# Ln and Exp of the first four rows done row by row instead of in pairs

## The chip, the cores and the metric

The kernel runs on one core of one Trainium2 chip. The metric is the device time of one execution in microseconds (us). Five runs of the kernel before gave a median of 169.43 us, from 169.14 to 169.55. A separate execution was recorded by the hardware profiler; it took 169.62 us.

## The reference

For every row of 1024 positive numbers the sum of the reciprocals is computed, over 32 x 512 rows:

```python
x: float32 [32, 512, 1024], |normal| + 1e-6
return np.sum(1.0 / x, axis=-1).astype(np.float32)
```

## The kernel before

The 16384 rows are spread over 128 partitions, 128 rows in each. What the kernel calls "row r" is therefore a tile of 128 x 1024 numbers, one matrix row in each partition, 512 KB. Rows 0 to 125 are treated whole; the last two, 126 and 127, are cut into two parts each, numbered 126 to 129.

The reciprocal is not computed element by element. A row has two halves a and b of 512 numbers. The kernel forms the product p = a b, then 1/p by two instructions on ScalarE, Ln with a scale and Exp of the negative, and uses 1/a + 1/b = (a + b) / (a b). So Ln and Exp run over 512 numbers per row rather than 1024. The steps of a row are tokens in a written-out plan (PLAN, line 37), a letter with the row's number. `+2` after it means two rows in one instruction, a pair, called a chain of two rows; `@` gives a slot or a bank. In the order of a row's life:

- **D** (line 185, SyncE's queue): loads so many further rows into a ring of 40 rows in SBUF. `D12 D15 D13` load rows 0 to 39 at the start. Every later load overwrites ring rows, and so waits until their readers and writers are done.
- **P** (line 197, GpSimd): the product of the halves, into a slot of the tile `prod` (22 slots of 512 numbers).
- **C** and **V** (lines 207 and 218): for some rows TensorE copies half b into a PSUM bank (matmul with the identity), and VectorE multiplies half a with it. This is the product without GpSimd. **W** is the same by VectorE alone.
- **S** (line 230, TensorE): adds the two halves into a PSUM bank, by two matmuls with the identity. Only for some rows.
- **L** (line 240, ScalarE): Ln of the product with scale 2^17, in place in its slots. `L0+2@0` treats rows 0 and 1 and sets their slots to 0 and 1; P and V read the slots from these tokens.
- **E** (line 249, ScalarE): Exp of minus that. With a bank, as in `E0+2@6`, the result goes to PSUM (here banks 6 and 7); without one it stays in its slot.
- **R** (line 265, VectorE): multiplies and sums. If the row has an S, it multiplies the sum in PSUM with 1/p in `prod` (128 x 512). Otherwise it multiplies both halves in the ring with 1/p in PSUM (128 x 1024). Each R is followed by a short instruction that reads out the accumulator, and the profile shows the two under the same line.

The order of tokens in the plan is the order of each engine's instructions; there is no other scheduler. Between engines the function `note` (line 133) records which ring rows, slots and banks each instruction reads and writes, and drops a wait where another wait already implies it.

For the first rows this means: rows 0 and 1 have P0+2 on GpSimd, and no S, so E0+2 writes to PSUM banks 6 and 7 and R0 and R1 read them there. Row 2 has P2 on GpSimd, row 3 has C3 and V3; both have an S (banks 0 and 1), so E2+2 stays in its slots. The next pair, rows 4 and 5, uses banks 6 and 7 again: E4+2@6 must wait until R0 and R1 have read them.

Of the kernel before, what the change touches and what calls it, by code (L numbers as in the profile page):

```python
# [11 lines left out]
def kernel(  # L12
# [22 lines left out]


    PLAN = """
        D12 D15 D13 P0+2 C3@3 S2@0 V3 P2 L0+2@0 C11@3 S3@1 E0+2@6 P4+2 V11 L2+2@2 R0 S6@2
        E2+2 R1 P6+2 L4+2@4 R2 R3 E4+2@6 S7@0 P8+2 L6+2@8 R4 S10@1 E6+2 R5 D7 P10 L8+2@10 R6
        R7 S11@2 E8+2@6 L10+2@6 R8 E10+2 R9 R10 R11 P12+2 C19@3 S14@0 V19 P14+2 L12+2@12  # L40
        S15@1 E12+2@6 S18@2 R12 P16+2 L14+2@16 R13 E14+2 R14 P18 L16+2@18 R15 S19@0 E16+2@6
        P20+2 L18+2@14 R16 D10 S22@1 E18+2 R17 P22+2 L20+2@20 R18 R19 E20+2@6 S23@2 P24+2
        L22+2@0 R20 S26@0 E22+2 R21 D7 P26 L24+2@2 R22 C27@3 R23 E24+2@6 P28+2 S27@1 V27 R24
        L26+2@4 C35@3 R25 E26+2 P30+2 S30@2 L28+2@8 V35 R26 E28+2@6 R27 S31@0 P32+2 L30+2@10
        R28 E30+2 S34@1 R29 D8 P34 L32+2@12 R30 R31 P36+2 E32+2@6 S35@2 L34+2@6 R32 C43@3
        E34+2 R33 P38+2 S38@0 L36+2@16 R34 R35 E36+2@6 S39@1 V43 P40+2 L38+2@18 R36 S42@2
        E38+2 R37 D8 P42 L40+2@20 R38 R39 E40+2@6 S43@0 P44+2 L42+2@14 R40 S46@1 E42+2 R41
        D4 L44+2@0 R42 R43 E44+2@6 P46+2 C51@3 R44 S47@0 V51 P48+2 L46+2@2 R45 S50@2 E46+2
        R46 P50 L48+2@8 R47 S51@1 E48+2@6 P52+2 L50+2@4 R48 S54@0 E50+2 R49 D6 P54+2 C59@3
        L52+2@10 R50 R51 E52+2@6 S55@2 V59 P56+2 L54+2@12 R52 S58@1 E54+2 R53 D6 P58  # L50
        L56+2@16 R54 R55 S59@0 E56+2@6 P60+2 L58+2@6 R56 S62@2 E58+2 R57 D4 P62+2 L60+2@18
        R58 R59 C67@3 E60+2@6 P64+2 S63@0 L62+2@20 V67 R60 E62+2 S66@1 R61 D4 P66 L64+2@14
        R62 E64+2@6 P68+2 R63 S67@2 L66+2@0 R64 E66+2 S70@0 R65 D3 P70+2 L68+2@2 R66 R67
# [259 lines left out]
```

## Time and profile before

| what | us |
|---|---|
| median of five runs (lowest, highest) | 169.43 (169.14, 169.55) |
| the profiled execution, its whole time | 169.62 |
| its span in the trace | 167.6 |
| TensorE busy | 132.1 |
| VectorE busy, 283 instructions | 128.2 |
| ScalarE busy, 157 instructions | 132.8 |
| GpSimd busy | 128.0 |
| load queue, share of 16 DMA engines' span | 94.6% |
| bytes read from HBM | 67.11 MB |

Busy time is the time in which an engine executes something. No engine's share of the span is over 79%, and the page lists for each group of instructions the idle time ahead of it and what ended it. The chain of waits follows the work that ended last back to the start; a releaser is inferred from semaphore events. Starts are counted from the beginning of the span, and lengths of successive instructions of one engine may overlap, so the distance of two starts is shorter than the length of the first.

### The profile page before, as it was taken

Reading aid. Unit: us, or ns where it says so; the run is one execution under the profiler, and the core shown is the slowest. Engines: PE = TensorE matmul, PEld = TensorE weight load, DVE = VectorE, ACT = ScalarE, POOL = GpSimd, SP = SyncE. Lnnn points to the kernel's source line nnn. Section 1 sums busy time; section 2 is a strip of 40 time slices with the busy share of each in tenths; the row PEclk is TensorE's granted clock in tenths of the full one; section 3 lists DMA queues with packets and bytes.
Section 4 is the critical chain, followed back from the end, with each engine's and each line's share of the span. In section 5 each row is a group of like instructions: output and inputs, shape, how many; then the busy total and the mean of one; then the engine's idle time right before and its main releaser. Section 6 shows DMA issues by size and latency. Waiting matters only on the chain.

```text
span 167.6 us, 1329 instructions
## 1 busy us (share of the span) xinstructions
PE 132.1 (79%) x292; PEld 54.6 (33%) x292; DVE 128.2 (76%) x283; ACT 132.8 (79%) x157; POOL 128.0 (76%) x80
## 2 busy tenths in 40 slices
PE   0000699929979999977998999999799679989691
PEld 0000243214433434322433434344244133434260
DVE  0000139853789989887798898799999999999993
ACT  3000096916999999976999997999899999999992
POOL 1000699129999999949999997966899997979960
PEclk9999999978999999999999999999999999999999
DMA  5998999999998998999999999999999999999910
GB/s 188 481 457 375 469 469 469 396 404 470 419 407 370 426 473 385 459 403 433 437 430 430 446 407 450 411 436 434 393 434 429 415 435 409 423 408 408 391 55 16
DMA packets 4615, 67.25 MB, mean 401 GB/s; under 512 B 512, under 2 KB 640, under 8 KB 2176
## 3 DMA queue, kind: packets, MB, share of 16 engines
q1 hardware_dynamic: 4608, 67.18, 94.6%
q8 instruction: 2, 0.03, 0.1%
q14 instruction: 5, 0.04, 0.1%
HBM read 67.11 MB, written 0.07 MB: 401 GB/s over the span
## 4 chain that ended last, share of the span: by engine, by line
DMA 50%; DVE 17%; POOL 11%; issue 8%; PE 8%; ACT 4%; DVEq 0%; SPq 0%; ACTq 0%; POOLq 0%
DMA ring<-in_x_dram 50%; POOL prod L197 11%; DVE ring L265 10%; PE ps L230 5%; DVE prod L265 4%; PE ps L207 3%; DVE prod L218 2%; ACT prod L240 2%; ACT ps L249 1%; DVE sums L265 1%; ACT prod L249 1%; DVEq L308 0%; SPq L185 0%; ACTq L240 0%; POOLq L197 0%
## 5 line engine op out<-in xcount | busy, mean ns | idle before, releaser
L197 POOL TENSOR_TENSOR prod<-ring 128x1024 f32<-128x1024 f32 (+2 forms) x74 | 127.3, 1754 | 34.0 <-DMA ring<-in_x_dram 29.1
L230 PE MATMUL ps<-ring,ident 128*128 128x512 f32 (+1 forms) x260 | 116.7, 595 | 5.5 <-DVE sums L265 4.3
L240 ACT ACTIVATE prod<-prod 128x1024 f32<-128x1024 f32 (+2 forms) x78 | 68.9, 893 | 28.0 <-POOL prod L197 27.1
L265 DVE CUSTOM_DVE_ANT_1 ring<-ring,ps 128x1024 f32<-128x1024 f32 (+1 forms) x65 | 76.4, 1209 | 8.4 <-ACT ps L249 8.4
L230 PEld LDWEIGHTS ps<-ring,ident 128*128 128x128 f32 x260 | 48.9, 193 | 72.9 <-issue 50.2
L265 DVE CUSTOM_DVE_ANT_0 prod<-prod,ps 128x512 f32<-128x512 f32 (+1 forms) x63 | 40.6, 679 | 1.2 <-ACT prod L249 1.2
L207 PE MATMUL ps<-ring,ident 128*128 128x512 f32 x32 | 18.9, 679 | 26.7 <-DMA ring<-in_x_dram 26.7
L249 ACT ACTIVATE ps<-prod 128x1024 f32<-128x1024 f32 (+2 forms) x39 | 33.8, 873 | 2.1 <-DVE sums L265 1.3
L249 ACT ACTIVATE prod<-prod 128x1024 f32<-128x1024 f32 (+2 forms) x39 | 34.5, 893 | 0.8
L218 DVE TENSOR_TENSOR prod<-ring,ps 128x512 f32<-128x512 f32 x16 | 10.9, 685 | 27.2 <-PE ps L207 27.0
L207 PEld LDWEIGHTS ps<-ring,ident 128*128 128x128 f32 x32 | 5.7, 204 | 36.3 <-issue 21.2
L265 DVE DVE_READ_ACCUMULATOR2_ANT sums<- 128x1 f32 x130 | 10.8, 83 | 0.0
L218 DVE TENSOR_TENSOR prod<-ring 128x512 f32<-128x512 f32 (+1 forms) x7 | 4.4, 658 | 0.0
L83 ACT ACT_TABLE_LOAD x1 | 1.3, 1283 | 0.7 <-PEq L297 0.7
L265 DVE CUSTOM_DVE_ANT_0 prod<-prod,ps,sums 128x256 f32<-128x256 f32 x2 | 0.9, 478 | 0.0
masks.py:197 POOL MEMSET ident<- 128x128 f32 x1 | 0.2, 205 | 0.3 <-POOLq L297 0.3
masks.py:199 POOL TENSOR_SCALAR_AFFINE_SELECT ident<-ident 128x128 f32<-128x128 f32 x1 | 0.3, 295 | 0.1
L297 POOL MEMSET const-float32-0.0<- 128x1 f32 x1 | 0.1, 99 | 0.2 <-issue 0.2
L297 POOL MEMSET const-bfloat16-1.0<- 128x1 bf16 x1 | 0.1, 102 | 0.0
L297 POOL MEMSET const-uint8-127<- 128x1 uint8 x1 | 0.1, 102 | 0.0
L297 POOL MEMSET const-float32-1.0<- 128x1 f32 x1 | 0.1, 99 | 0.0
## 6 DMA issues: line engine op xcount, KB each, us to landing
ring<-in_x_dram SPq DMA_DIRECT2D x2, 4096.0 KB, 32.3
ring<-in_x_dram SPq DMA_DIRECT2D x1, 7680.0 KB, 35.2
ring<-in_x_dram SPq DMA_DIRECT2D x2, 3584.0 KB, 30.5
ring<-in_x_dram SPq DMA_DIRECT2D x1, 6656.0 KB, 50.5
ring<-in_x_dram SPq DMA_DIRECT2D x1, 6144.0 KB, 17.5
ring<-in_x_dram SPq DMA_DIRECT2D x3, 2048.0 KB, 34.7
ring<-in_x_dram SPq DMA_DIRECT2D x2, 3072.0 KB, 32.4
ring<-in_x_dram SPq DMA_DIRECT2D x1, 5120.0 KB, 27.2
```

The costliest lines, as they stand in the source:

```text
L83: nc.scalar.add_instruction(mybir.InstLoadActFuncSet(name=nc.get_next_instruction_name(), act_func_set_id=act_sets.index("natural_log_exp_ ...
L197: inst = nc.gpsimd.tensor_tensor(out=prod[:, p : p + m, :w], in0=ring[:, a : a + m, at : at + w], in1=ring[:, a : a + m, at + w : at + 2 * w],
L207: inst = nc.tensor.matmul(ps[:, b, : place(r)[2]], lhsT=ident, rhs=xs(r, 1), start=True, stop=True,)
L218: inst = nc.vector.tensor_tensor(out=prod[:, p, :w], in0=xs(r, 0), in1=in1, op=mult)
L230: inst = nc.tensor.matmul(ps[:, b, : place(r)[2]], lhsT=ident, rhs=xs(r, h), start=h == 0, stop=h == 1,)
L240: inst = nc.scalar.activation(out=pg, in_=pg, func=Ln, scale=S)
L249: inst = nc.scalar.activation(out=rc, in_=pg, func=Exp, scale=-1.0)
L265: inst = nc.vector.tensor_tensor_reduce(out=row, in0=row, in1=other, scale=S, scalar=total if q in summed else 0.0, op0=mult, op1=add, acc ...
L297: nc = _bacc.Bacc("TRN2", target_bir_lowering=False, num_devices=1)
```

## The change

In the plan, L0+2, E0+2, L2+2 and E2+2 are replaced by instructions for one row each. Rows 0 and 1 keep their slots (0, 1) and banks (6, 7). Row 2 gets slot 3 and row 3 slot 2, where they had 2 and 3. P0+2 stays one instruction for two rows. The rest of the plan holds the same tokens in the same order; its lines are only broken elsewhere. The announcement of the change says that ScalarE has three instructions more; in the diff, eight tokens stand for four.

```diff
-        D12 D15 D13 P0+2 C3@3 S2@0 V3 P2 L0+2@0 C11@3 S3@1 E0+2@6 P4+2 V11 L2+2@2 R0 S6@2
-        E2+2 R1 P6+2 L4+2@4 R2 R3 E4+2@6 S7@0 P8+2 L6+2@8 R4 S10@1 E6+2 R5 D7 P10 L8+2@10 R6
...
+        D12 D15 D13 P0+2 C3@3 S2@0 V3 P2 L0@0 L1@1 C11@3 S3@1 E0@6 E1@7 P4+2 V11 L2@3 L3@2
+        R0 S6@2 E2 E3 R1 P6+2 L4+2@4 R2 R3 E4+2@6 S7@0 P8+2 L6+2@8 R4 S10@1 E6+2 R5 D7 P10
...
```

More of the change, by code (lines that the diff above doesn't have):

```diff
@@ L37 @@
     PLAN = """
-        D12 D15 D13 P0+2 C3@3 S2@0 V3 P2 L0+2@0 C11@3 S3@1 E0+2@6 P4+2 V11 L2+2@2 R0 S6@2
-        E2+2 R1 P6+2 L4+2@4 R2 R3 E4+2@6 S7@0 P8+2 L6+2@8 R4 S10@1 E6+2 R5 D7 P10 L8+2@10 R6
[L40 to L49, printed above, removed]
@@ L50 @@
-        L52+2@10 R50 R51 E52+2@6 S55@2 V59 P56+2 L54+2@12 R52 S58@1 E54+2 R53 D6 P58
+        D12 D15 D13 P0+2 C3@3 S2@0 V3 P2 L0@0 L1@1 C11@3 S3@1 E0@6 E1@7 P4+2 V11 L2@3 L3@2
+        R0 S6@2 E2 E3 R1 P6+2 L4+2@4 R2 R3 E4+2@6 S7@0 P8+2 L6+2@8 R4 S10@1 E6+2 R5 D7 P10
+        L8+2@10 R6 R7 S11@2 E8+2@6 L10+2@6 R8 E10+2 R9 R10 R11 P12+2 C19@3 S14@0 V19 P14+2
+        L12+2@12 S15@1 E12+2@6 S18@2 R12 P16+2 L14+2@16 R13 E14+2 R14 P18 L16+2@18 R15 S19@0
+        E16+2@6 P20+2 L18+2@14 R16 D10 S22@1 E18+2 R17 P22+2 L20+2@20 R18 R19 E20+2@6 S23@2
@@ new lines @@
+        P24+2 L22+2@0 R20 S26@0 E22+2 R21 D7 P26 L24+2@2 R22 C27@3 R23 E24+2@6 P28+2 S27@1
+        V27 R24 L26+2@4 C35@3 R25 E26+2 P30+2 S30@2 L28+2@8 V35 R26 E28+2@6 R27 S31@0 P32+2
+        L30+2@10 R28 E30+2 S34@1 R29 D8 P34 L32+2@12 R30 R31 P36+2 E32+2@6 S35@2 L34+2@6 R32
+        C43@3 E34+2 R33 P38+2 S38@0 L36+2@16 R34 R35 E36+2@6 S39@1 V43 P40+2 L38+2@18 R36
+        S42@2 E38+2 R37 D8 P42 L40+2@20 R38 R39 E40+2@6 S43@0 P44+2 L42+2@14 R40 S46@1 E42+2
+        R41 D4 L44+2@0 R42 R43 E44+2@6 P46+2 C51@3 R44 S47@0 V51 P48+2 L46+2@2 R45 S50@2
@@ L51 @@
+        E46+2 R46 P50 L48+2@8 R47 S51@1 E48+2@6 P52+2 L50+2@4 R48 S54@0 E50+2 R49 D6 P54+2
+        C59@3 L52+2@10 R50 R51 E52+2@6 S55@2 V59 P56+2 L54+2@12 R52 S58@1 E54+2 R53 D6 P58
         L56+2@16 R54 R55 S59@0 E56+2@6 P60+2 L58+2@6 R56 S62@2 E58+2 R57 D4 P62+2 L60+2@18
```

## The prediction

> **What bounds the kernel now.** I read the page first, then the chain of waits, the timelines of ScalarE, VectorE and SyncE over the first 50 us, and the waits inside the stretch that the edit touches. The page's slices and queue table say that the stream of x sets the pace:
>
> ```profile
> DMA  5998999999998998999999999999999999999910
> ...
> q1 hardware_dynamic: 4608, 67.18, 94.6%
> ```
>
> The DMA engines are nearly full from the second slice to the 38th. The chain of waits (start, length, what) shows where the first stretch of compute stand against that stream:
>
> ```profile
> 0.74 17.47 DMA ring<-in_x_dram
> 18.21 0.07 issue
> 18.28 11.78 POOL prod L197 x6
> 30.07 6.39 issue
> ...
> 36.48 7.00 POOL prod L197 x3
> ```
>
> Rows 0 to 11 (D12) land at 18.28. GpSimd multiplies its share of them until 30.07 and then has nothing until 36.46, when rows 12 to 26 (D15) land. So rows 0 to 11 form an island: their work starts on a landing and is followed by a second landing that was issued before any compute. The changed instructions are the first eight on this island. Next, ScalarE's timeline (start, length, instruction, idle before it and its releaser):
>
> ```profile
> 20.66 1.06 ACT L240 ACTIVATE prod<-prod 128x1024 f32<-128x1024 f32 x1 [18.64 <-POOL prod L197]
> 21.75 1.03 ACT L249 ACTIVATE ps<-prod 128x1024 f32<-128x1024 f32 x1
> 22.71 1.04 ACT L240 ACTIVATE prod<-prod 128x1024 f32<-128x1024 f32 x1
> 23.78 1.06 ACT L249 ACTIVATE prod<-prod 128x1024 f32<-128x1024 f32 x1
> 24.75 1.04 ACT L240 ACTIVATE prod<-prod 128x1024 f32<-128x1024 f32 x1
> 27.06 1.03 ACT L249 ACTIVATE ps<-prod 128x1024 f32<-128x1024 f32 x1 [1.27 <-DVE sums L265]
> ...
> 33.17 1.06 ACT L249 ACTIVATE prod<-prod 128x1024 f32<-128x1024 f32 x1
> 38.86 1.06 ACT L240 ACTIVATE prod<-prod 128x1024 f32<-128x1024 f32 x1 [4.64 <-POOL prod L197]
> ```
>
> These are L0+2, E0+2, L2+2, E2+2, L4+2, E4+2, then E10+2 and L12+2. Two things to see: E4+2 stands still for 1.27 us, because its banks 6 and 7 are still read by R0 and R1 on VectorE; and after E10+2 ScalarE idles 4.64 us. VectorE's timeline tells why R0 and R1 come when they do, and how its own island ends:
>
> ```profile
> 20.43 0.69 DVE L218 TENSOR_TENSOR prod<-ring,ps 128x512 f32<-128x512 f32 x1 [20.43 <-PE ps L207]
> 24.00 0.69 DVE L218 TENSOR_TENSOR prod<-ring,ps 128x512 f32<-128x512 f32 x1 [2.88 <-PE ps L207]
> 24.61 1.21 DVE L265 CUSTOM_DVE_ANT_1 ring<-ring,ps 128x1024 f32<-128x1024 f32 x1
> ...
> 35.70 0.08 DVE L265 DVE_READ_ACCUMULATOR2_ANT sums<- 128x1 f32 x1
> 38.57 0.69 DVE L218 TENSOR_TENSOR prod<-ring,ps 128x512 f32<-128x512 f32 x1 [2.79 <-PE ps L207]
> ```
>
> V3 runs at 20.43, V11 at 24.00 as soon as TensorE's copy C11 is there, R0 directly behind V11 at 24.61. R0 needs E0, but E0+2 is over at 22.78 (21.75 + 1.03), 1.83 us before R0 starts: what holds R0 is V11 ahead of it, and that is held by TensorE, which the edit does not touch.
>
> **The change, part by part.** The plan's tokens L0+2, E0+2, L2+2, E2+2 become L0, L1, E0, E1, L2, L3, E2, E3. That is eight instructions for four, so four more on ScalarE (the diff counts; the announced three does not fit it). Row 2's product moves to slot 3 and row 3's to slot 2. The order of all other engines stays, and no transfer moves.
>
> *Added ScalarE time.* The price of a half-size instruction is in the later part of the same timeline, where rows go one by one. One 128x512 starts 0.52 us after its predecessor when it does not read its result (149.57, 150.09, 150.61), and 0.65 us after when it does (150.61 to 151.26). The double ones start 0.96 us after an independent one (21.75 to 22.71) and 1.09 or 1.07 us after their own input (20.66 to 21.75, 22.71 to 23.78). Before, L0+2 to L4+2 take 24.75 - 20.66 = 4.09 us (1.09 + 0.96 + 1.07 + 0.97). After, no instruction reads its direct predecessor's result, so eight steps of 0.52 or 0.53 make 4.16 to 4.24 us. The added time is about 0.1 us: four times 0.08 us (2 x 0.52 - 0.96) for the splits, less twice some 0.12 us of the dependent steps that go. The high end, by mean durations laid end to end, is 4 x 0.2 = 0.8 us (2 x 0.619 - 1.047 = 0.19 for Ln, 2 x 0.62 - 1.054 = 0.19 and 2 x 0.584 - 1.025 = 0.14 for Exp); it ignores the overlap that the start times show. The low end is zero. I take 0.1 us, since the start times are rows of just these instructions.
>
> [...]
>
> *What covers it.* L4+2 starts at about 24.86 rather than 24.75 and ends at 25.90. E4+2 cannot start before 27.06, since R1 ends just before. So the wait of 1.27 us shrinks to 1.16 us, and from E4+2 on ScalarE is where it was. At the high end (0.8 us) 0.47 us of it still remains. Without that wait the 0.1 us would go on through E6+2, E8+2 to R8, which does wait for ScalarE (0.48 us), and would end VectorE's island at 35.88 instead of 35.78; V19 comes at 38.57 whatever happens, behind D15 and C19. That is a second cover of 2.79 us. (TensorE's S7, S10 and S11 wait for R2, R3 and R6 to free their banks and would come later by as much; TensorE's own idle time ahead of D15 is 3.32 us in its timeline.) So the edit must cost more than 1.27 + 2.79 = 4.06 us, about 1 us for each added instruction, before anything after the island moves.
>
> *Rows that finish earlier or later.* L0 starts at 20.66, L1 at 21.18, E0 at 21.71, E1 at 22.23, L2 at 22.76, L3 at 23.29, E2 at 23.81, E3 at 24.34, which ends at 24.96. E0 is done at 22.3 rather than 22.78: worth nothing, as R0 stands behind V11 until 24.61. E3 is done 0.1 us later than E2+2 was; R3 asks for it at 27.49, so 2.5 us are spare. L2 needs P2 on GpSimd, which is over at about 21.9 (18.28 + 2.37 + 1.28), and L3 needs V3, over at 21.12; both lie ahead of 22.76.
>
> *Added waits.* R1 now waits for E1 itself and R3 for E3, where one wait for the pair had served; both were fulfilled microseconds before. No trace row shows a fulfilled wait by itself. The nearest gaps are ahead of reductions on VectorE: 0.00 us for most, 0.02 us (28.10 to 28.12), 0.05 us (43.30 to 43.35). I take 0.02 us each, with bounds of 0 and 0.05; below zero it cannot be, as nothing is removed. Behind R1 stand R2 and R3 on VectorE and E4+2 on ScalarE, which would pass at most 0.1 us on, into the 2.79 us.
>
> *SyncE's queue.* D7 refills ring rows 0 to 6 and waits for the last of R0, R1, R4 and R5. SyncE's timeline and its wait in that stretch:
>
> ```profile
> 30.60 0.33 SPq L185 DMA_DIRECT2D ring<-in_x_dram  x1
> ```
>
> ```profile
> SPq L185 <- DVE sums L265: 28.4, 1, 28.4
> ```
>
> The load ahead of it (D13, 6656 KB) was issued by 1.8 us and needs 50.5 us to land, so D7 has some 21 us in hand. A shift of 0.1 us in R5 cannot starve the stream.
>
> *Sum.* The profiled execution took 169.62 us, of which the span is 167.6 and 2.0 lies around it; the median of the runs is 169.43, 0.19 lower. 169.62 + 0.1 (ScalarE) + 0.04 (two waits) - 0.14 (both covered) = 169.62, and on the median's scale 169.43.
>
> **The rivals.**
>
> *Slower: ScalarE's longer program is fetched late.* The edit leaves the work of the rest of the kernel alone, yet shifts every later ScalarE instruction by four places in its program. The page counts seven instruction packets (queues 8 and 14, 0.07 MB). If one of them came too late, it would hurt where ScalarE has no room: from 92.34 to 135.20 us it is busy 40.84 of 42.86 us. The price, by the nearest row, is that of one small transfer, the output's 64 KB with 1.5 us to landing: 169.43 + 1.5 = 170.9; the 2.0 us of idle time in that stretch may swallow part of it, so 169.8 to 170.9. It decides only once a packet comes later than the last instruction of the one before. Against it: in the trace of before, no ScalarE wait is of this kind; the engine waits for GpSimd, VectorE and, 0.7 us at the start, for the launch. Chance 0.07.
>
> *Faster: rows released singly start the reductions earlier.* E0 ends about 0.48 us earlier. If R0 followed it and the refill D7 were what the stream waits for, all of that would come through: 168.95. Against it stand V11's 2.88 us wait for TensorE, right ahead of R0, and D7's 21 us in hand. Chance 0.05.
>
> *The change is not what it says, or its waits go elsewhere.* Swapped slots 2 and 3 could tie a later product to the wrong row; but the next user of these slots is P24+2, after 36 us, when R2 and R3 have been over since 28.18. Extra waits at their high end give 0.1 us, under the cover: still 169.43. This belongs to the forecast.
>
> **How the numbers follow.** No change 0.88, with 169.43 as the likeliest; slower 0.07; faster 0.05. About 0.2%, 0.34 us, is what a measurement of this kernel can tell from no change; the five runs spread over 169.14 to 169.55. The covered costs add nothing to the range even at their high ends (0.8 + 0.1 us against 4.06), so its width is the spread of the runs about the median (-0.29, +0.12), taken somewhat wider for a median on another occasion and reaching to the edge of each rival: 168.95 is the faster one's time, 169.9 the lower part of the slower one's.
>
> **What would show each step right or wrong.** In the profile of the changed kernel ScalarE should have 161 instructions, eight of 128x512 from about 20.66 with starts 0.52 apart; L4+2 at about 24.86; the wait before E4+2 about 1.16 us with E4+2 at 27.06; VectorE's last accumulator read on the island near 35.7 to 35.8; D7 issued near 30.6; the POOL wait until about 36.46 as before. I am wrong if E4+2 starts without a wait, if any engine's wait for D15 is gone, or if ScalarE shows an idle time later on that no engine or transfer releases.

## The result and the profile after

The changed kernel has a median of 169.42 us over 48 runs (168.88 to 170.52). The kernel before, over 89 runs, has 169.63 us. The ratio is 0.9987, with a 95% interval of 0.9982 to 0.9992. The time lies in the forecast's range and moved by less than the 0.2% named there, but the interval leaves out 1: by this comparison the kernel became 0.22 us faster, where "no change" was forecast. (In what follows, means leave out single runs that lie some 2 us above all others.)

On the island, rows 0 to 11, the profile of the changed kernel looks as forecast. First the chain of waits (start, length, what):

```profile
0.74 17.48 DMA ring<-in_x_dram
18.30 11.77 POOL prod L197 x6
30.07 6.36 issue
36.45 7.01 POOL prod L197 x3
```

The second landing ends GpSimd's wait at 36.45, where it was 36.48. Next ScalarE's timeline:

```profile
20.67 1.15 ACT L240 ACTIVATE prod<-prod 128x512 f32<-128x512 f32 x2 [18.65 <-POOL prod L197]
21.73 1.10 ACT L249 ACTIVATE ps<-prod 128x512 f32<-128x512 f32 x2
22.77 1.13 ACT L240 ACTIVATE prod<-prod 128x512 f32<-128x512 f32 x2
23.80 1.13 ACT L249 ACTIVATE prod<-prod 128x512 f32<-128x512 f32 x2
24.84 1.04 ACT L240 ACTIVATE prod<-prod 128x1024 f32<-128x1024 f32 x1
27.45 1.03 ACT L249 ACTIVATE ps<-prod 128x1024 f32<-128x1024 f32 x1 [1.56 <-DVE sums L265]
...
33.55 1.06 ACT L249 ACTIVATE prod<-prod 128x1024 f32<-128x1024 f32 x1
38.83 1.06 ACT L240 ACTIVATE prod<-prod 128x1024 f32<-128x1024 f32 x1 [4.22 <-POOL prod L197]
```

L0+2 to L4+2 took 4.09 us before; the eight single instructions take 24.84 - 20.67 = 4.17 us. The split costs 0.08 us of ScalarE's time, and E4+2 still stands still after it. It starts later than forecast, at 27.45, and VectorE's timeline says why:

```profile
24.38 0.69 DVE L218 TENSOR_TENSOR prod<-ring,ps 128x512 f32<-128x512 f32 x1 [3.25 <-PE ps L207]
24.98 1.21 DVE L265 CUSTOM_DVE_ANT_1 ring<-ring,ps 128x1024 f32<-128x1024 f32 x1
...
36.09 0.08 DVE L265 DVE_READ_ACCUMULATOR2_ANT sums<- 128x1 f32 x1
38.34 0.69 DVE L218 TENSOR_TENSOR prod<-ring,ps 128x512 f32<-128x512 f32 x1 [2.17 <-PE ps L207]
```

V11 waited for TensorE until 24.38 instead of 24.00, so R0 and all that follows it on the island is some 0.38 us late, and the cover of 2.79 us swallows that. TensorE's first sums took longer this time. Here is the row of before and, next, of the changed kernel:

```profile
20.18 2.92 PE L230 MATMUL ps<-ring,ident 128*128 128x512 f32 x4
```

```profile
20.20 3.29 PE L230 MATMUL ps<-ring,ident 128*128 128x512 f32 x4
```

In both traces TensorE's first matmuls behind the landing take 1.06 us or more each (four before, five after the change), the next one 0.78 and 0.73 us, and the next ten 0.59 us each; the first of these ten starts at 22.51 us before and at 23.32 after. In six profiles of the kernel before (this one and the five copies below) V11 starts anywhere from 23.30 to 24.84 us; in five of the changed kernel it starts from 23.54 to 24.65. So the 0.38 us are within what one kernel does by itself, and nothing ties them to the edit.

So the first 36 us gave nothing away and gained nothing. Where, then, do the profiles differ? At the very end. After the last result SyncE sends the output, and then the engines drain and exchange semaphores, with two releases (line 308, the end of the program; GpSimd's instructions that give them start at 166.84 and 167.50 us before, at 166.70 and 167.18 after). From the last VectorE instruction to the end of the span it took 167.607 - 165.013 = 2.594 us before, and 167.279 - 164.885 = 2.394 us after. These are the sequencers' last DRAIN instructions at that line, in the last microsecond (number, lengths in ns, first and last start), of before:

```profile
L308 DVEq DRAIN  x1: 19/19/19, 167.0 to 167.0; - x1
...
L308 ACTq DRAIN  x1: 127/127/127, 167.3 to 167.3; - x1
```

and of the changed kernel:

```profile
L308 ACTq DRAIN  x1: 14/14/14, 166.8 to 166.8; - x1
L308 DVEq DRAIN  x1: 19/19/19, 166.9 to 166.9; - x1
```

At the first release the waits of SyncE, ScalarE, VectorE and TensorE end within 0.012 us of each other (166.880 to 166.892 us before, 166.743 to 166.754 after). Before, ScalarE's DRAIN comes at 167.265, 0.381 us after the instruction that ends its wait (166.884), and takes 127 ns. After, it comes 0.091 us behind (166.747 to 166.838) and takes 14 ns. VectorE's gap is 0.11 us in both. GpSimd's next instruction waits for the semaphore that these DRAINs update: before it starts at 167.424 us, 0.032 us behind the end of ScalarE's DRAIN and 0.268 us after the start of GpSimd's own last one; after the change it starts 0.079 us after that one; the difference of 0.19 us is nearly the whole difference of the two ends. The profile shows no semaphore and no other engine that accounts for ScalarE's delay. The page's queue table shows one thing more, the packets of the kind "instruction"; this is the row of before and, next, of the changed kernel:

```profile
q14 instruction: 5, 0.04, 0.1%
```

```profile
q14 instruction: 6, 0.05, 0.1%
```

A packet of 8192 bytes that came at 167.93 us, just beyond the end of the span, in before, has no counterpart there in the changed kernel; that one has a packet at 159.77 us instead. So theory B was formed: the delay belongs to one place in the order of ScalarE's instructions, and in the kernel before this place lies between the last wait and the last DRAIN. The change adds four ACTIVATEs and removes one separate wait (L2+2 needed GpSimd and VectorE, L2 and L3 need one each), three places in all (ScalarE has 193 records in the trace of before and 196 in that of the changed kernel). That fits the "three more" of the announcement, and by theory B it moves the end away from the place of the delay. Theory A: the split itself gains. Theory C: the kernel gains nothing that the time shows, and the ratio is in the comparison.

### The profile page after: what moved, and what is told of

The parts are those of the page before. It is cut to its first block, busy times and chain, and to the rows that moved or that the text cites. A ratio compares the mean times of both kernels' runs of the same rounds, so it can differ in the third digit from the quotient of the medians.

```text
span 167.3 us, 1332 instructions
## 1 busy us (share of the span) xinstructions
PE 132.5 (79%) x292; PEld 54.8 (33%) x292; DVE 128.0 (77%) x283; ACT 132.9 (79%) x161; POOL 128.0 (77%) x80
## 4 chain that ended last, share of the span: by engine, by line
DMA 50%; DVE 17%; POOL 11%; issue 8%; PE 8%; ACT 4%; DVEq 0%; SPq 0%; ACTq 0%; POOLq 0%
DMA ring<-in_x_dram 50%; POOL prod L197 11%; DVE ring L265 10%; PE ps L230 5%; DVE prod L265 4%; PE ps L207 3%; DVE prod L218 2%; ACT prod L240 2%; ACT ps L249 1%; DVE sums L265 1%; ACT prod L249 1%; DVEq L308 0%; SPq L185 0%; ACTq L240 0%; POOLq L197 0%
```

## The experiments

All were made on one core as the change was. "End" is the time from the last VectorE instruction to the end of the span, from the trace.

**e1: the kernel before, against itself.** No edit.

> The kernel before, unchanged, timed against itself: the noise of the comparison. Every theory expects a ratio of 1.000 with an interval that holds 1, within about 0.0006 to either side. Theory B (the last stretch of ScalarE's program) also expects that ScalarE's last DRAIN again comes late after the final exchange: in the profile of before it starts at 167.265 us, 0.38 us after the wait at 166.884, where VectorE's comes 0.11 us after its own; if the 0.38 us is gone here, B falls.

Ratio 0.9992 (0.9983 to 1.0000). End 2.587 us, ScalarE's last DRAIN 0.365 us after its wait. The DRAIN was as theory B has it. The ratio was not 1 within 0.0006, which points to theory C.

**e2: three tiny instructions ahead, pairs kept.**

```diff
     make_identity(nc, ident)
+    small = pool.tile([P, 256], f32)
+    for i in range(3):
+        nc.scalar.activation(out=small[0:1, i : i + 1], in_=ident[0:1, 0:1],
+                             func=mybir.ActivationFunctionType.Ln)
```

> The pairs stay as before; ScalarE gets three tiny Ln instructions (one number each) before the first load has landed, where it idles until 20.66 us, so its whole program stands three places further on, as in the changed kernel (196 ScalarE records in the trace of after, 193 in that of before). Theory A (the split of rows 0 to 3 is what gains): ratio 1.000, 169.63 us, last DRAIN 0.38 us late. Theory B (the gain is that the end of ScalarE's program stands elsewhere in its instruction stream): ratio 0.9987, 169.42 us as after, last DRAIN within 0.10 us of the wait, span about 0.2 us shorter after the last VectorE instruction (2.39 instead of 2.59 us).

Ratio 0.9988 (0.9979 to 0.9996), mean 169.344 us. End 2.403 us. The last DRAIN, of this kernel:

```profile
L315 ACTq DRAIN  x1: 14/14/14, 167.0 to 167.0; - x1
```

It takes 14 ns and comes 0.092 us after its wait, as in the changed kernel. No row is split here, so the shorter end does not need the split: for the end, theory A falls.

**e3: 128 tiny instructions ahead.** As e2, with `range(128)`.

> Pairs as before, 128 tiny Ln instructions ahead (at some 0.1 us each they fit into the 18 us of waiting). Theory B, if what matters is the place within blocks of 128 instructions (the instruction packets of the trace have 8192 bytes): the end stands in the same place of its block as before, so ratio 1.000 and the last DRAIN 0.3 to 0.4 us late. If any longer program gained: 0.9987. Theory A: 1.000 too, but it says nothing of the DRAIN.

Ratio 0.9993 (0.9982 to 1.0003), mean 169.405 us. End 2.608 us, DRAIN 0.376 us late:

```profile
L315 ACTq DRAIN  x1: 142/142/142, 166.8 to 166.8; - x1
```

Three more places take the DRAIN from 0.381 to 0.092 us behind its wait, 128 take it back to 0.376. So a longer program is not enough to remove the stall. That ScalarE's instructions come in blocks is not shown; shown is that 128 places more bring the stall back and 127 (e8) do not. ScalarE's timeline also shows what the tiny ones cost, 12.05 us for 128, inside the wait for the first rows:

```profile
2.03 12.05 ACT L104 ACTIVATE small<-ident 1x1 f32<-1x1 f32 x128
```

**e4: the change, with 125 tiny instructions ahead.** `range(125)` in the changed kernel.

> The changed kernel (rows 0 to 3 one by one) with 125 tiny Ln instructions ahead: with the three that the split adds, 128 places further on than before. Theory A (the split gains): 0.9987, as after. Theory B (the place of the end): 1.000, the last DRAIN late again by 0.3 to 0.4 us, although the split is there.

Ratio 0.9990 (0.9981 to 0.9999), mean 169.389 us. End 2.587 us, DRAIN 0.366 us late. The split is there and the stall too. With e2 this closes the square: the end took 2.594 and 2.587 us with none and with 128 places more (before, e4), and 2.403 and 2.394 us with three (e2, the changed kernel), each time once without the split and once with it. The ratio 0.9990 is not the 1.000 that theory B expected, but the copy of before in e1 is as far from 1.

**e5 and e6: the changed kernel and a copy of before, measured together.**

> The changed kernel once more, beside another copy of the kernel before, on one chip. Theory B (place of the end of ScalarE's program): from the last VectorE instruction to the end of the span 2.39 to 2.40 us, and a median some 0.2 us below that of the copy of before in this call (ratio of the two about 0.9988). Theory C (no real gain, the ratio of 0.9987 is how the runs of one kernel scatter): the two medians agree within 0.1 us.

> The kernel before against itself once more, since the first such run gave 0.9992 where 1.000 was expected. Theory B: 2.59 us from the last VectorE instruction to the end, ratio 1.000 within 0.0008. Theory C: another ratio between 0.999 and 1.001, no nearer to 1 than that of the changed kernel.

The changed kernel: ratio 0.9977 (0.9965 to 0.9988), mean 169.263 us of 7 runs, end 2.401 us. The copy of before: ratio 0.9986 (0.9977 to 0.9995), mean 169.433 us of 11, end 2.584 us. The difference of the means, 0.17 us, favours theory B. Yet here a kernel is "faster than itself" by 0.14%, with an interval that leaves out 1. The recorded ratio of the change itself, 0.9987, is no further from 1.

**e7: one tiny instruction ahead.** `range(1)`.

> Pairs as before and one tiny Ln ahead: ScalarE's program one place further on. Theory B: the stall sits at one place of the stream, in before between the wait at 166.884 and the DRAIN at 167.265; one place further on it falls ahead of that wait, where ScalarE stands still for 2.9 us anyway, so the end comes 2.39 to 2.40 us after the last VectorE instruction. If it needs two or three places, 2.59 us. Theory A: 2.59 us, since no row is split.

One run, 169.12 us. The DRAIN was prompt (0.091 us), but the end took 2.581 us, where theory B expected 2.39 to 2.40 us. The delay sat elsewhere, on SyncE's wait for the output, of this kernel and of the next one:

```profile
SPq L315 <- DMA out_dram<-sums: 1.1, 1, 1.1
```

```profile
SPq L315 <- DMA out_dram<-sums: 0.9, 1, 0.9
```

In the trace of e7 an instruction packet starts at 165.20 us, while the output is under way (issued at 164.79, landed after 1.7 us, where it took 1.5 us in e8). That the packet held up the output is not shown.

**e8: 127 tiny instructions ahead.** `range(127)`.

> Pairs as before and 127 tiny Ln ahead: by blocks of 128 the program stands one place earlier than before. Theory B: the stall moves behind the last DRAIN, ahead of ScalarE's very last wait; that DRAIN is then prompt (0.1 us after the wait before it), GpSimd's exchange is not held up (0.08 us after its DRAIN instead of 0.27), and only ScalarE's own last wait can come late, by up to 0.3 us: from the last VectorE instruction to the end 2.4 to 2.6 us. Theory A: 2.59 us, DRAIN late as in before.

One run, 169.27 us. DRAIN prompt (0.092 us), end 2.397 us; GpSimd goes on 0.079 us after its DRAIN. With one instruction fewer than in e3 the DRAIN comes 0.092 us behind its wait instead of 0.376, with one more than before (e7) 0.091 instead of 0.381.

In the kernel before, the packet of 8192 bytes at 167.93 us starts 0.66 us behind the start of the late DRAIN (167.265). With 127 tiny instructions (e8) one starts between 167.7 and 167.8 us, some 0.6 to 0.7 us behind ScalarE's next instruction, its last wait, at 167.1. So the packet follows the late DRAIN in the one and the instruction behind the DRAIN in the other. But in the kernel before it comes after the late DRAIN and not ahead of it, so the DRAIN did not wait for this packet. What ScalarE did in the 0.29 us that the DRAIN was late (0.381 less the 0.091 us of the changed kernel) is not shown.

**e9 to e12: a copy of before, the changed kernel, 128 and 127 tiny ones, measured together.**

> A third copy of the kernel before, to be set against the other three of this call and not only against its own reference, since two copies of it had ratios of 0.9992 and 0.9986 to themselves. Theory B: 2.59 us from the last VectorE instruction to the end; mean about 169.41 us, as the 44 runs so far of kernels whose last DRAIN is late. Theory C (no real gain in the time): the same mean as the next one within 0.05 us.

> The changed kernel a third time. Theory B: 2.39 to 2.40 us to the end, and a mean 0.1 to 0.2 us below that of the copy of before in this call. Theory C: no difference over 0.05 us.

> 128 tiny Ln instructions ahead of the pairs, as before. Theory B: stall, 2.59 us to the end, mean as the copy of before in this call. Any theory in which a longer ScalarE program gains by itself: as the changed kernel.

> One tiny Ln fewer than in the last one, and nothing else changed; no row is split. Theory B: no stall, 2.40 us to the end, mean 0.1 to 0.2 us below the one with 128, level with the changed kernel. Theory A (the split gains) and theory C: the same mean as with 128, within 0.05 us.

| run | ratio (95%) | mean us, 11 runs | end us |
|---|---|---|---|
| e9, before | 0.9991 (0.9981 to 1.0000) | 169.363 | 2.596 |
| e10, changed | 0.9993 (0.9984 to 1.0002) | 169.435 | 2.401 |
| e11, 128 tiny | 0.9990 (0.9981 to 0.9999) | 169.401 | 2.582 |
| e12, 127 tiny | 0.9996 (0.9987 to 1.0005) | 169.434 | 2.395 |

The ends are as theory B says, to 0.02 us. The times are not: the changed kernel is 0.07 us above the copy of before. Here theory C has it.

**e13 to e16: two changed ones against two copies of before, measured together.** Asked: does a gain of 0.19 us reach the time?

> Theory B with the whole gain coming through: mean 0.19 us below those of the two copies of before in this call. Theory C (what the end gains is not seen in the time): within 0.07 us of them, and a ratio between 0.9985 and 0.9997 like theirs. The profile shows 2.39 to 2.40 us to the end by both.

> Copy of before. Theory B: ratio of 1.000 or the 0.999 of the earlier copies, and a mean 0.19 us above the two changed ones of this call. Theory C: level with them. The profile shows 2.58 to 2.60 us to the end by both.

> As the first changed one of this call; the two together make 22 runs. Theory B: 0.19 us below the copies of before. Theory C: level with them within 0.07 us.

> As the first copy of before in this call; the two together make 22 runs. Theory B: 0.19 us above the changed ones. Theory C: level with them within 0.07 us.

Ratios 0.9993 (0.9977 to 1.0009) and 0.9987 (0.9972 to 1.0003) for the changed ones, 0.9995 (0.9979 to 1.0011) and 0.9992 (0.9979 to 1.0006) for the copies of before. Means 169.458 us (22 runs, standard error 0.064) and 169.517 us (24 runs, 0.036): a difference of 0.06 us with a standard error of 0.07. That is within theory C's 0.07 us, though these runs alone cannot quite exclude theory B's 0.19. Ends 2.393 and 2.397 against 2.588 and 2.591 us.

**All together.** Four sums over the runs:

- The reference runs of the kernel before, taken beside the experiments, have a mean of 169.562 us (115 runs, standard error 0.021); its copies e1, e6, e9, e14 and e16 have 169.448 us (57 runs, 0.025). The same program comes out 0.11 us, 0.07%, lower when it stands in the place of the kernel under study. Some 0.09 us of it lie inside the span (167.48 against 167.40 us). Why is not known. About half of the 0.22 us that were recorded for the change is of this size.
- Where both were measured together, the changed copies have 169.417 us (40 runs, 0.042) and those of before 169.460 us (46 runs, 0.028): the change is worth 0.04 us with a standard error of 0.05.
- All kernels with the late DRAIN (e1, e3, e4, e6, e9, e11, e14, e16) have 169.430 us (90 runs, 0.019), those with the prompt one (e2, e5, e10, e12, e13, e15) 169.407 us (62 runs, 0.030): 0.02 us with a standard error of 0.04.
- The split by itself shows nothing in the time when the end is alike. With the late DRAIN e4 (split) has 169.389 us, e1 and e3 (pairs) 169.397 and 169.405; with the prompt one e10 (split) has 169.435 and e12 (pairs) 169.434 us, each with a standard error of 0.04 to 0.06. For the time, too, theory A has nothing in its favour.

So the stall at the end is real in every profile (2.58 to 2.61 us with it in nine, before, e1, e3, e4, e6, e9, e11, e14 and e16; 2.39 to 2.40 us without it in eight; e7, with a prompt DRAIN and 2.58 us, is the exception), and little or nothing of its 0.19 us is found in the time. In the span, as the runs list it, the two groups differ by 0.07 us (167.377 and 167.306), with a standard error of 0.03; outside the span the kernels with the prompt DRAIN spend 2.10 us and the others 2.05. Where the rest goes stays open: the last VectorE instruction comes at 164.60 to 165.09 us in the profiles, a scatter more than twice the stall.

## Why the prediction was right or wrong

- **ScalarE's added time.** Right: 0.1 us taken, 0.08 us found; start times of single instructions in the later part of the trace were the right rows.
- **The first cover.** Right in kind. The wait before E4+2 was forecast to shrink to 1.16 us; it is 1.56 us, because V11 came 0.38 us late. I had taken TensorE's 24.00 us for a fixed time, but it moves between executions of one kernel, from 23.30 to 24.84 us in six profiles.
- **The second cover and D15.** Right. GpSimd's second landing is where it was, and V19 starts at 38.34 us (38.57 before), behind a wait of 2.17 us that is still there. D7 went out at 30.98 instead of 30.60 us, against the 21 us it had in hand.
- **Added waits.** One separate wait is gone, which I did not see: L2 and L3 share the two releasers of L2+2. I counted four more instructions where the announcement's three was the net number of places.
- **The sum.** This is the step that failed. It has no term for the 2.59 us behind the last VectorE instruction: I set them down as unchanged without reading them, since the chain of waits ends at that instruction and the waits list nothing of ScalarE's sequencer there. There lay a stall of 0.19 us that the edit removed: 2.39 to 2.40 us in every profile of the changed kernel, 2.58 to 2.61 in every one of the kernel before. How much of the recorded 0.22 us comes from it stays open, since copies of the kernel before show about half of that gain as well.
- **The time itself.** That 169.42 us was measured where 169.43 was forecast is luck. The forecast stands on the median of five runs, and that lay 0.20 us below the median of the 89 runs against which the change was measured. I also took 0.34 us for the least that a measurement can tell from no change; the interval of the recorded comparison is 0.0010 of the time wide, about 0.17 us.
- **The rival of the fetched program.** Its premise came near: with ScalarE's program three places longer, its last DRAIN came 0.09 us behind the wait instead of 0.38. Its sign was wrong, and its cause is not shown. I asked only whether a longer program might be fetched at a worse place, and argued that no ScalarE wait of this kind is in the trace of before. It was there, in the last DRAIN of line 308. Its price is 0.19 us at the end, not 1.5 us in the middle, and the packet nearest to it starts 0.66 us behind the late DRAIN, so a late packet, as I had it, is not what the traces show.
- **The rival of earlier reductions.** Rightly refused: R0 came at 24.98, not earlier.
- **No change.** Against copies of the same kernel the change is worth 0.04 us with a standard error of 0.05, well under the 0.34 us that I named as the limit. By that the forecast holds; by the interval of the recorded comparison it does not, and about half of that comparison's gain shows in copies of the kernel before as well.

## What to carry to other kernels

Before work between two landings of a full stream is given a price, look at the idle time ahead of the next landing: here 0.08 us more on ScalarE did not delay the work on the second landing (GpSimd went on at 36.45 us, 36.48 before), and VectorE had 2.79 us of idle time ahead of V19. Read the stretch behind the last result too, sequencer by sequencer, when a few tenths of a microsecond are at stake: here three places more in ScalarE's program went with an end of 2.39 instead of 2.59 us, whether rows were split (the changed kernel) or not (e2, 2.40). And before a gain of 0.1% is put down to an edit, time a copy of the old kernel in the place of the new one.

## What had not been expected of the hardware

ScalarE's last DRAIN came 0.38 us behind the wait ahead of it in the kernel before and with 128 tiny instructions ahead (e3), and 0.09 us behind it with one, three and 127 (e7, e2, e8). What ScalarE did in the difference is not shown. Its tiny instructions went at 12.05 / 128 = 0.094 us each (e3). And with one and the same program V11, which follows TensorE's first three steps, started anywhere from 23.30 us (e1) to 24.84 us (e6), though GpSimd's first product started at 18.13 us in the one and at 18.22 us in the other.
